# Turning SwiGLU's activation tiles with transposing transfers inside SBUF, with a reordered quad of weight sums and put-together steps set apart

## The chip, the cores and the metric

The kernel runs on one core of a Trainium2 chip. The metric is device time in microseconds of one execution, from launch to the last output. A core has five engines with a queue of instructions each, which run in order and wait for each other by semaphores: TensorE (PE; its weight loads are shown apart as PEld), VectorE (DVE), ScalarE (ACT), GpSimd (POOL) and SyncE (SP). Sixteen DMA engines move data between HBM and the on-chip memory SBUF, or inside SBUF; transfers are issued from the queues of SP, POOL and, rarely, ACT. TensorE writes its results to PSUM, eight banks of 128 x 512 float32.

## The reference

One layer of a decoder for 256 tokens of width 2048, all in float32. What surrounds the change is the SwiGLU feed-forward part (`D_FF` = 5632):

```python
h = rms_norm(x, g_ffn_pre[layer])
gate, up = jnp.split(h @ w_gate_up[layer], 2, axis=-1)
x = x + rms_norm((jax.nn.silu(gate) * up) @ w_down[layer], g_ffn_post[layer])
```

Before it stand a mixer (an input product `w_in` of sliding-window attention, a linear recurrence and two sigmoid gates, two branch products and `w_out`), after it a gated embedding (`w_ple_gate`). Every one of these is a product of 256 tokens with a weight matrix from HBM.

## The kernel before

The 256 tokens are two halves c = 0, 1 of 128. A product is made from blocks of 512 output columns, with the activation (turned, so that its 128-row groups k lie on the partitions) as the stationary operand and 128 x 512 pieces of the weights as the moving one. To get float32 accuracy, each operand is split into a rounded high part and a remainder, and `terms` (L473) makes three matmuls: high by high, low by high, high by low. So each weight piece that comes from HBM needs an ACT copy (`hi`, tile `wh`) and a DVE subtraction (`lo`, tile `wl`) before PE can use it.

The weights are loaded by SP in pairs (two row groups, 512 KB) in an order that `plan_of_weights` (L82) writes out. Two consecutive pairs, those of the same rows for two blocks of columns, form a quad. A quad is used in one of two ways. As usual it takes 2 x 2 x 2 products of three matmuls, 24 in all. A quad marked "seven" goes through seven products instead of eight (a Strassen-like scheme over the two row groups, the two token halves and the two blocks), 21 matmuls: `parts_of_quad` (L364) makes four sums t1 to t4 of weights on DVE and seven hi/lo splits, `in_place_of_quad` (L594) the sums on the side of the activation, and `by_quads` (L520) runs the products in the order b11, b21, t1, t2, b22, t4, t3. Four of the seven go to accumulators of their own (`sums`), which `put_together` (L567) combines after the last such quad of a block into four tiles u (one ACT copy `p1`, four DVE sums); `total` (L585) then adds each accumulator of the block to its u and frees the bank. During such a block all eight PSUM banks are in use: four accumulators and four sums.

In the gate/up stage, `swiglu(j)` (L1621) runs over eleven blocks j of 512 columns of gate and 512 of up. Block 0 is done in the plain way; j = 1 to 10 by quads, with four "seven" quads in blocks 2, 4, 6, 8, three in blocks 3, 5, 7, 9 and two in blocks 1 and 10 (`quads_of_block`, L61). At a block's end, for each half c, the gate's total goes through Silu on ACT, the up's total is multiplied by it on DVE, and `gated` (L1609) turns the resulting tile of 128 tokens x 512 columns, which must become four 128 x 128 groups with columns on the partitions: `transpose4` (L656) asks `misc` (L270) for a bank, which waits until at least three of the eight are free, and runs four PE transposes into it; ACT copies the bank to `actT`, and SP stores it to HBM (`actd`). During the `w_down` stage, `act_parts` (L1671) loads these tiles again through POOL's queue and splits them. `by_quads` and `put_together` are also used for two thirds of the gate columns of `w_in` (`gate_pair`, L1380), for half of `w_out`, and for `w_down`.

The order of the instructions on every queue is made by a small planner while the program is written. A clock advances with each matmul (0.227 us for one of 512 columns, 0.11 for a small one); `InOrder` (L154) estimates when DVE and ACT would be done with what they have been given (`until`). Work around the matmuls is written as generators: `yield T`, `yield A`, `yield V` ask to go on after that engine's planned end, `yield 0.5` after so much planned time, and `pump` (L219) resumes those that are due after each matmul group. `hurry` (L223) resumes them ahead of time when a bank or a tile is needed at once. `prefetch_quads` (L434) keeps at least two split weight items ready, or DVE planned 1.5 us ahead, as long as ten of the 61 SBUF slots (128 x 512 float32 each) are free. The planner's estimates only fix the order; on the chip the engines wait by semaphores.

Of the kernel before, what the change touches and what calls it, by code (L numbers as in the profile page):

```python
# [13 lines left out]
F32 = mybir.dt.float32  # L14
F32R = mybir.dt.float32r
I32 = mybir.dt.int32
AF = mybir.ActivationFunctionType
ALU = mybir.AluOpType
AX = mybir.AxisListType

P = 128
D = 2048
NB = 512
# [6 lines left out]

TABLES = (AF.Sigmoid, AF.Silu, AF.Exp, AF.Ln, AF.Sin)
TABLE_LOAD = 1.3
# [96 lines left out]
def block_kernel(ctx: ExitStack, tc: tile.TileContext, I, out: bass.AP):  # L129
# [24 lines left out]
    class InOrder:  # L154
# [20 lines left out]
        def __getattr__(self, name):  # L175
            f = getattr(self.engine, name)

            def call(o, *a, **kw):
                if name != "dma_start":
                    self.estimate(name, o, a, kw)  # L180
                return tc.keep_in_program_order(f(o, *a, **kw))  # L181

            return call

    V = InOrder(nc.vector, 0.07, 0.00105)
    A = InOrder(nc.scalar, 0.16, 0.0008)
    G, T, S = InOrder(nc.gpsimd, 0.9, 0.002), InOrder(nc.tensor, 0.0, 0.0), InOrder(nc.sync, 0.0, 0.0)
# [9 lines left out]
    def transpose(o, i, idn):  # L197
        clock[0] += SMALL
        T.transpose(o, i, idn)
# [29 lines left out]
    def nm(s):  # L229
        count[0] += 1  # L230
        return f"{s}_{count[0]}"
# [4 lines left out]
    def slot(s, shape=(P, NB), dt=F32):  # L236
        i = free_slots.popleft()
        t = slots.tile(list(shape), dt, tag=f"s{i}", name=nm(s))
        owner[id(t)] = i, t
        return t  # L240

    def free(*tiles):
        for t in tiles:
            free_slots.append(owner.pop(id(t))[0])

    def room(n):

        while len(free_slots) < n:
            yield 0.3
# [13 lines left out]
    def drop(ps):  # L263
        banks.append(bank_of.pop(id(ps))[0])
# [5 lines left out]
    def misc():  # L270
        while len(banks) < 3:
            yield 0.3
        return bank("misc")

    def act(o, i, f, **kw):
        return A.activation(o, i, f, **kw)

    def tt(o, a, b, op):
        return V.tensor_tensor(o, a, b, op)
# [12 lines left out]
    def cols(h, d=P):  # L292
        return slice(h * d, (h + 1) * d)
# [21 lines left out]
    def split_pair():  # L315
# [3 lines left out]
        if isinstance(raw, list):  # L319
            parts = [(slot("wh", dt=F32R), slot("wl", dt=F32R)) for j in range(2)]  # L320
            for (hi, lo), r in zip(parts, raw):
                act(hi, r, AF.Copy)
                tt(lo, r, hi.bitcast(F32), ALU.subtract)
            done = partial(free, *parts[0], *parts[1])
            free(*raw)
        elif len(in_pool) < SPLIT + 1:
            hi = wsplit.tile([P, 2, NB], F32R, tag="wh", name=nm("wh"))
            lo = wsplit.tile([P, 2, NB], F32R, tag="wl", name=nm("wl"))
            act(hi, raw, AF.Copy)
            tt(lo, raw, hi.bitcast(F32), ALU.subtract)  # L330
            parts, done = [(hi[:, j, :], lo[:, j, :]) for j in range(2)], in_pool.popleft
            in_pool.append(k)
        else:
            parts = [(slot("wh", dt=F32R), slot("wl", dt=F32R)) for j in range(2)]
            for j in range(2):
                act(parts[j][0], raw[:, j, :], AF.Copy)
            for j in range(2):
# [4 lines left out]
    def parts_of_pair():  # L342

        w, k, col, raw, _ = loaded.popleft()
        if len(in_pool) <= SPLIT:
            hi = wsplit.tile([P, 2, NB], F32R, tag="wh", name=nm("wh"))
            lo = wsplit.tile([P, 2, NB], F32R, tag="wl", name=nm("wl"))
            in_pool.append(k)
            act(hi, raw, AF.Copy)
            yield  # L350
            tt(lo, raw, hi.bitcast(F32), ALU.subtract)
            parts, done = [(hi[:, j, :], lo[:, j, :]) for j in range(2)], in_pool.popleft
        else:
            parts = [(slot("wh", dt=F32R), slot("wl", dt=F32R)) for j in range(2)]
            for j in range(2):
                act(parts[j][0], raw[:, j, :], AF.Copy)
            yield
# [6 lines left out]
    def parts_of_quad():  # L364

        w, k, col, raw, _ = loaded.popleft()
        other = loaded.popleft()[3]
        b11, b21, b12, b22 = raw[:, 0, :], raw[:, 1, :], other[:, 0, :], other[:, 1, :]
        parts = {}

        def hi(name, src):
            parts[name] = slot("wh", dt=F32R)
            act(parts[name], src, AF.Copy)

        def total(a, b, op):
            t = slot("t")
            tt(t, a, b, op)
            return t

        def lo(name, src):  # L380
            h, t = parts[name], slot("wl", dt=F32R)
            tt(t, src, h.bitcast(F32), ALU.subtract)
            parts[name] = h, t

        hi("b11", b11)
        hi("b21", b21)
        yield
        t1 = total(b11, b12, ALU.subtract)
        hi("t1", t1)
        lo("b11", b11)  # L390
        yield
        t2 = total(b22, t1, ALU.add)
        hi("t2", t2)
        t4 = total(b21, t2, ALU.subtract)
        hi("t4", t4)
        yield
        lo("b21", b21)
        load_more()
        t3 = total(b22, b12, ALU.subtract)
        hi("b22", b22)  # L400
        yield
        hi("t3", t3)
        lo("t1", t1)
        lo("b22", b22)
        load_more()
        free(t1)
        yield
        lo("t2", t2)
        lo("t4", t4)
        free(t2, t4)  # L410
        yield
        lo("t3", t3)
        free(t3)
        ready.append(((w, k, col), parts, None))

    def load_more():
        if plan:
            load_pair()
# [3 lines left out]
    def begin():  # L422

        if not loaded or len(making) > 1:
            return
        if loaded[0][4]:
            if len(loaded) > 1 and len(free_slots) >= STEP + SPARE:
                making.append(parts_of_quad())
                next(making[-1])
        elif len(in_pool) <= SPLIT or len(free_slots) >= ROOMY:  # L430
            making.append(parts_of_pair())
            next(making[-1])
# [87 lines left out]
    def by_quads(w, n, order, lhs, sides, cs, sums, us, start=True, stop=True, evac=None):  # L520
# [4 lines left out]
        for i, (q, seven) in enumerate(order):  # L525
# [38 lines left out]
            if last:  # L564
                chain(put_together(sums, us))

    def put_together(sums, us):  # L567

        yield T
        yield from room(4)  # L570
        p1, u2, u3, u4 = (slot("u") for _ in range(4))
        act(p1, sums["b11"], AF.Copy)
        drop(sums["b11"])
        yield A
        tt(u2, sums["t2"], p1, ALU.add)
        drop(sums["t2"])
        tt(u4, sums["t1"], u2, ALU.add)
        yield V
        tt(u3, sums["t3"], u2, ALU.add)
        drop(sums["t3"])  # L580
        tt(u2, sums["t1"], u3, ALU.add)
        drop(sums["t1"])
        us.extend([[p1, u3], [u4, u2]])

    def total(us, n, c, ps):  # L585
# [43 lines left out]
    def lookup(groups):  # L629
        def there(g):  # L630
            return g in groups if isinstance(groups, dict) else len(groups) > g and groups[g] is not None

        def f(k):
            hurry(lambda: there(k // 4))
            hi, lo = groups[k // 4]
            return hi[:, k % 4, :], lo[:, k % 4, :]
        f.groups = groups
        return f
# [17 lines left out]
    def transpose4(src):  # L656
        ps = yield from misc()
        for i in range(4):
            transpose(ps[:, cols(i)], src[:, cols(i)], ident)
        return ps  # L660
# [146 lines left out]
    sinks = amask[:, 256:272]  # L807
    posi = cst.tile([P, 2], I32, name="posi")

# [223 lines left out]
    def hgrn_core(c, g):  # L1033
# [55 lines left out]
        def scores(lev):  # L1089
# [22 lines left out]
            if lev < 5:  # L1112
                V.copy_predicated(
                    right(sc),
                    cmask[:, cols(lev, 64)].rearrange("p (n w) -> p n w", w=w).unsqueeze(1)
                    .broadcast_to([P, 4, nb, w]).bitcast(I32),
                    pv.rearrange("p h (n w) -> p h n w", w=w))
# [488 lines left out]
    stored, parts, sides, down_sides = [set(), set()], [], {}, {}  # L1606
    h2T = [lookup(n.groups) for n in norm2]

    def gated(c, j, t):  # L1609

        pa = yield from transpose4(t)
        free(t)
        yield T
        at = slot("actT")
        act(at, pa, AF.Copy)
        drop(pa)
        S.dma_start(actd[c][j], at)
        free(at)
        stored[c].add(j)

    def swiglu(j):  # L1621
# [16 lines left out]
        def ev_u(c, ps):  # L1638
            def f():
                if j in BY_QUADS and SEVEN:  # L1640
                    t = yield from total(us, 1, c, ps)
                    while sg[c] is None:
                        yield 0.3
                    yield sg[c]
                    stt(t, t, norm2[c].r, sg[c], ALU.mult, ALU.mult)
                    free(sg[c])
                else:
                    while sg[c] is None:
                        yield 0.3
                    t = sg[c]  # L1650
                    stt(t, ps, norm2[c].r, t, ALU.mult, ALU.mult)
                    drop(ps)
                yield V
                yield from gated(c, j, t)
            chain(f())
# [57 lines left out]
    for at, (pair, gi) in enumerate(DOWN):  # L1713
        if at % 5 == 0:
            ps, us = [[acc(), acc()] for n in range(2)], []
            sums = {"left": len(SEVEN_DOWN[pair])}
# [138 lines left out]
```

## Time and profile before

| | |
|---|---|
| three runs | 1487.32, 1487.96, 1491.14 us; median 1487.96 |
| the profiled execution | 1489.56 us, its span 1487.5 us |
| granted TensorE clock | 0.997 of full speed |
| busy: PE, DVE, ACT, POOL | 99%, 83%, 60%, 4% of the span |
| weights and other HBM reads | 298.08 MB, 211 GB/s over the span with the writes |
| the 22 tiles `actT` | first copied at 731.5 us, last at 1160.9 us |

The span counts from the first to the last recorded instruction; the execution's own time is about 2 us longer. The mean duration of one instruction is its time from start to end; since engines begin the next instruction before the last one has left the pipeline, the busy time of a group of back-to-back instructions is less than count times mean. In a group's row, "idle before" is the time that the engine stood still just ahead of these instructions, with what released it. All helpers record their instructions under one line, L181, so groups are told apart by engine and tile: `acc` are accumulators, `misc` banks for transposes and small products, `raw` weights as loaded, `wh` and `wl` their parts, `shi` and `slo` the parts of sums of activations, `t` sums of weights, `u` what put-together makes.

### The profile page before, as it was taken

What the parts mean: (1) busy time and instruction counts of PE and PEld (TensorE: products, weight loads), DVE (VectorE), ACT (ScalarE), POOL (GpSimd) and SP (SyncE); (2) the same over time, 40 slices, a digit from 0 to 9 for tenths busy, and PEclk for the clock granted to TensorE, in tenths of its full rate; (3) what the DMA queues carried; (4) which work ended last, traced back from release to release, by engine and by line L of the source; (5) the groups of instructions that cost most, each with busy time, mean ns of one, the idle gap of its engine ahead of it and who ended that gap; (6) DMA issues with size and microseconds to landing.
All of it is one profiled execution on the core that took longest, in us unless ns stands there. A gap on an engine that the chain in (4) does not pass through costs nothing.

```text
span 1487.5 us, 19958 instructions
## 1 busy us (share of the span) xinstructions
PE 1469.5 (99%) x6838; PEld 1216.3 (82%) x6838; DVE 1239.9 (83%) x2043; ACT 888.9 (60%) x1417; POOL 62.9 (4%) x107
## 2 busy tenths in 40 slices
PE   9999999999999999999999999999999999999997
PEld 6888888888887888888888888888888887888885
DVE  6878958755999867977899999999988899997773
ACT  7755655566666645665655666565655666575661
POOL 2100000000000100000000000000000000010000
PEclk9999999999999999999999999999999999999998
DMA  9754544345576856866756676576677678797551
GB/s 342 257 188 155 171 141 128 114 128 170 184 240 227 309 185 201 272 227 199 252 182 219 205 238 213 174 230 206 215 239 268 214 252 270 214 336 260 192 188 56
DMA packets 159557, 314.59 MB, mean 211 GB/s; under 512 B 11072, under 2 KB 11520, under 8 KB 159456
## 3 DMA queue, kind: packets, MB, share of 16 engines
q1 hardware_dynamic: 153024, 293.38, 61.0%
q0 software_dynamic: 6256, 19.88, 3.7%
q8 instruction: 53, 0.87, 0.2%
q14 instruction: 48, 0.39, 0.1%
q10 hardware_dynamic: 176, 0.07, 0.0%
HBM read 298.08 MB, written 15.21 MB: 211 GB/s over the span
## 4 chain that ended last, share of the span: by engine, by line
PE 64%; DVE 4%; issue 2%; DMA 1%; ACT 1%; DVEq 0%; POOLq 0%; POOL 0%; ACTq 0%
PE acc L181 63%; DVE wl L181 2%; PE misc L181 1%; DVE u L181 1%; ACT wh L181 1%; DVE t L181 1%; DMA raw<-in_w_in 1%; DMA raw<-in_w_down 0%; DMA raw<-in_w_gate_up 0%; DVE eg L181 0%; DVE slo L181 0%; DVE lo L181 0%; ACT hi L181 0%; DVE sides L181 0%; DVE s L181 0%
## 5 line engine op out<-in xcount | busy, mean ns | idle before, releaser
L181 PE MATMUL acc<-wh,hi 128*128 128x512 f32 x1769 | 700.2, 396 | 3.6 <-DVE u L181 2.4
L181 DVE TENSOR_TENSOR wl<-raw,wh 128x1024 fp32r<-128x1024 f32 (+1 forms) x606 | 595.7, 1007 | 115.4 <-ACT wh L181 113.8
L181 PE MATMUL acc<-wl,hi 128*128 128x512 f32 x1769 | 690.0, 390 | 0.0
L181 PE MATMUL acc<-wh,lo 128*128 128x512 f32 x1769 | 688.9, 389 | 0.0
L181 ACT ACTIVATE wh<-raw 128x1024 fp32r<-128x1024 f32 (+1 forms) x606 | 514.3, 883 | 239.8 <-PE acc L181 101.6
L181 PEld LDWEIGHTS acc<-wl,hi 128*128 128x128 f32 x1769 | 332.0, 188 | 71.2 <-DVE wl L181 1.1
L181 PEld LDWEIGHTS acc<-wh,hi 128*128 128x128 f32 x1769 | 332.3, 188 | 70.6 <-DVE u L181 3.2
L181 PEld LDWEIGHTS acc<-wh,lo 128*128 128x128 f32 x1769 | 332.5, 188 | 66.6 <-issue 0.2
L181 ACT ACTIVATE wh<-t 128x512 fp32r<-128x512 f32 x236 | 145.6, 628 | 106.6 <-DVE t L181 85.9
L181 DVE TENSOR_TENSOR wl<-t,wh 128x512 fp32r<-128x512 f32 x236 | 152.2, 683 | 0.5 <-PE acc L181 0.5
L181 DVE TENSOR_TENSOR u<-acc,u 128x512 f32<-128x512 f32 x132 | 86.3, 684 | 18.8 <-PE acc L181 17.6
L181 PE MATMUL acc<-wh,shi 128*128 128x512 f32 x236 | 91.9, 390 | 1.2 <-ACT shi L181 1.2
L181 PE MATMUL acc<-wh,slo 128*128 128x512 f32 x236 | 91.9, 390 | 0.2 <-DVE slo L181 0.2
L181 PE MATMUL acc<-wl,shi 128*128 128x512 f32 x236 | 91.8, 389 | 0.0
L181 DVE TENSOR_TENSOR t<-raw,t 128x512 f32<-128x512 f32 x118 | 81.1, 687 | 3.7
L181 PEld LDWEIGHTS acc<-wh,shi 128*128 128x128 f32 x236 | 44.3, 188 | 10.8 <-ACT shi L181 1.6
L181 PEld LDWEIGHTS acc<-wh,slo 128*128 128x128 f32 x236 | 44.3, 188 | 9.7 <-DVE slo L181 0.5
L181 PEld LDWEIGHTS acc<-wl,shi 128*128 128x128 f32 x236 | 44.3, 188 | 9.2
L181 POOL DMA_DIRECT2D act<-actd x40 | 21.4, 538 | 601.9 <-DVE wl L181 402.4
L181 DVE TENSOR_TENSOR t<-raw,raw 128x512 f32<-128x512 f32 x59 | 40.3, 684 | 3.9 <-DMA raw<-in_w_gate_up 1.9
L181 DVE TENSOR_TENSOR t<-raw 128x512 f32<-128x512 f32 x59 | 40.3, 684 | 0.0
L181 DVE TENSOR_TENSOR lo<-act,hi 128x512 fp32r<-128x512 f32 x40 | 27.2, 684 | 8.1 <-ACT hi L181 8.0
(214 smaller groups left out, 852.1 us busy)
## 6 DMA issues: line engine op xcount, KB each, us to landing
raw<-in_w_gate_up SPq DMA_DIRECT2D x176, 512.0 KB, 4.6
raw<-in_w_in SPq DMA_DIRECT2D x152, 512.0 KB, 4.3
raw<-in_w_down SPq DMA_DIRECT2D x88, 512.0 KB, 5.5
raw<-in_w_out SPq DMA_DIRECT2D x32, 512.0 KB, 5.5
raw<-in_w_ple_gate SPq DMA_DIRECT2D x32, 512.0 KB, 5.1
act<-actd POOLq DMA_DIRECT2D x40, 256.0 KB, 5.6
raw<-in_w_attn_branch SPq DMA_DIRECT2D x16, 512.0 KB, 5.2
raw<-in_w_hgrn_branch SPq DMA_DIRECT2D x16, 512.0 KB, 5.1
```

Source lines behind the costliest of these rows:

```text
L181: return tc.keep_in_program_order(f(o, *a, **kw))
```

## The change

It has three parts.

1. `gated` no longer uses PE and PSUM. ACT copies the tile, read as 16-bit halves, into a tile `apart` with all low halves first and all high halves after them (1024 two-byte elements per partition). ACT's queue issues one transposing transfer from SBUF to SBUF, which turns the eight 128 x 128 squares of halves into `turned`. After 7.0 us of planned time ACT copies the halves back together into `actT`; SP's store is now issued after ACT's planned end instead of at once. The input tile is freed as soon as `apart` has been written, without waiting for banks. The planner leaves transfers of either kind out of its estimates.
2. In `parts_of_quad`, the low part of b21 is made ahead of the sum t4 and its high part, instead of behind them and behind a pause.
3. In `put_together`, the four DVE sums are set apart by two planned pauses of 0.5 us where one pause lasted until DVE's planned end; the last u is t3 + u4 in place of t1 + u3, which is the same sum, so the bank of t1 is freed after the second sum and that of t3 after the fourth.

```diff
@@ class InOrder, call
-                if name != "dma_start":
+                if not name.startswith("dma_start"):
                     self.estimate(name, o, a, kw)
@@ parts_of_quad
         t2 = total(b22, t1, ALU.add)
         hi("t2", t2)
+        lo("b21", b21)
+        yield
         t4 = total(b21, t2, ALU.subtract)
         hi("t4", t4)
-        yield
-        lo("b21", b21)
         load_more()
@@ put_together
         tt(u2, sums["t2"], p1, ALU.add)
         drop(sums["t2"])
+        yield 0.5
         tt(u4, sums["t1"], u2, ALU.add)
-        yield V
+        drop(sums["t1"])
         tt(u3, sums["t3"], u2, ALU.add)
+        yield 0.5
+        tt(u2, sums["t3"], u4, ALU.add)
         drop(sums["t3"])
-        tt(u2, sums["t1"], u3, ALU.add)
-        drop(sums["t1"])
         us.extend([[p1, u3], [u4, u2]])
@@ gated
+    def halves(t):
+
+        return t.bitcast(U16).rearrange("p (n two) -> p two n", two=2)
+
     def gated(c, j, t):
 
-        pa = yield from transpose4(t)
+        apart = slot("apart", (P, 2 * NB), U16)
+        act(apart.rearrange("p (two n) -> p two n", two=2), halves(t), AF.Copy)
         free(t)
-        yield T
+        turned = slot("turned", (P, 8, P), U16)
+        A.dma_start_transpose(turned, apart)
+        free(apart)
+        yield 7.0
         at = slot("actT")
-        act(at, pa, AF.Copy)
-        drop(pa)
+        act(halves(at), turned.rearrange("p (two c) t -> p two (c t)", two=2), AF.Copy)
+        free(turned)
+        yield A
         S.dma_start(actd[c][j], at)
```

More of the change, by code (lines that the diff above doesn't have):

```diff
@@ L16 @@
 I32 = mybir.dt.int32
+U16 = mybir.dt.uint16
 AF = mybir.ActivationFunctionType
```

## The prediction

> **What bounds the kernel now.** I read the page's busy times first, then the groups of instructions for what TensorE waits on, then the chain, then the windows of the gate/up stage.
>
> ```profile
> span 1487.5 us, 19958 instructions
> PE 1469.5 (99%) x6838; PEld 1216.3 (82%) x6838; DVE 1239.9 (83%) x2043; ACT 888.9 (60%) x1417; POOL 62.9 (4%) x107
> L181 PE MATMUL acc<-wh,hi 128*128 128x512 f32 x1769 | 700.2, 396 | 3.6 <-DVE u L181 2.4
> ```
>
> TensorE (PE) is busy for 1469.5 of 1487.5 us; of the 18.0 us that are left, its largest matmul group waited only 3.6 us, 2.4 of them for VectorE (DVE) sums named u. So what leaves PE's stream leaves the time, as long as the engines that feed it keep up. Do they? Four blocks of the gate/up stage (those with four reordered quads, j = 2, 4, 6, 8), and the sum of ten windows of about a block each:
>
> ```profile
> 771.00:814.00 43.00, 43.00 (x191) 35.63 (x190) 41.19 (x59) 25.39 (x37) 0.00 (x0) 1.00 0.63 196
> 856.00:899.00 43.00, 43.00 (x195) 35.49 (x193) 41.17 (x60) 26.87 (x40) 0.00 (x0) 1.00 0.74 232
> 940.00:984.00 44.00, 44.00 (x199) 36.20 (x197) 42.58 (x62) 26.88 (x40) 0.00 (x0) 1.00 0.71 227
> 1025.00:1068.00 43.00, 43.00 (x196) 35.65 (x195) 41.73 (x60) 26.87 (x40) 0.00 (x0) 1.00 0.72 232
> sum 430.00, PE 429.54 PEld 355.09 DVE 401.77 ACT 258.35 POOL 5.38; mean PE 42.95 PEld 35.51 DVE 40.18 ACT 25.84 POOL 0.54
> ```
>
> Columns: window, length, busy time of PE, weight loads, DVE, ACT, POOL, then granted clock, share of the DMA engines, GB/s. PE is idle for 0.46 us in 430. DVE has 401.77 (93%), and in the blocks of four quads 41.2 of 43 to 42.6 of 44: no more than about 2 us behind PE. ACT has 60%, the DMA engines 63 to 74% in these blocks. PE bounds, DVE is close.
>
> **Term 1: the transposes leave PE.** Each of 22 activation tiles (11 blocks, 2 token halves) was turned by four PE transposes, 88 in all. A tile waits for three free banks, and a block holds all eight, so both halves' eight run together at a block's end. On the timeline and on the chain:
>
> ```profile
> 724.73 0.39 PE L181 MATMUL acc<-wh,hi 128*128 128x512 f32 x1
> ...
> 727.45 0.39 PE L181 MATMUL acc<-wh,hi 128*128 128x512 f32 x1
> ...
> 729.26 0.39 PE L181 MATMUL acc<-wl,hi 128*128 128x512 f32 x1
> 729.49 1.03 PE L181 MATMUL misc<-ident,sg 128*128 128x128 f32 x8
> 730.28 0.48 PE L181 MATMUL acc<-wh,hi 128*128 128x512 f32 x1
> 730.60 0.40 PE L181 MATMUL acc<-wh,lo 128*128 128x512 f32 x1
> ```
> ```profile
> 729.65 0.87 PE misc L181 x8
> ...
> 814.90 0.97 PE misc L181 x8
> ...
> 899.55 1.25 PE misc L181 x8
> ...
> 984.07 1.26 PE misc L181 x8
> ...
> 1068.57 1.11 PE misc L181 x8
> ...
> 1157.93 0.87 PE misc L181 x8
> ```
>
> A matmul starts every (727.45 - 724.73) / 12 = 0.227 us. Eight transposes take 730.28 - 729.49 = 0.79 us, and the first matmul after them is followed 0.32 us later instead of 0.227, so a group moves PE's stream by about 0.89 us. On the chain the eleven groups (shown are the first, the last and the four longest; the rest are 0.87 or 0.88) are 0.87 to 1.26 us each and sum to 10.7; the long ones hold a wait on a bank. Eleven times 0.89 is 9.8; counting the overlap with the next matmul, the groups' busy times sum to 12.1:
>
> ```profile
> L181 PE MATMUL misc<-ident,u 128*128 128x128 f32 x80 | 11.1, 277 | 0.5 <-DVE u L181 0.4
> L181 PE MATMUL misc<-ident,sg 128*128 128x128 f32 x8 | 1.0, 272 | 0.0
> L181 ACT ACTIVATE actT<-misc 128x512 f32<-128x512 f32 x22 | 12.5, 595 | 34.9 <-PE misc L181 34.9
> ```
>
> Bounds 9.8 and 12.1; I take the chain's 10.7, since the waits on a bank go with the transposes.
>
> **Term 2: ScalarE (ACT) gets more.** Out go 22 copies of 595 ns from PSUM, and 34.9 us in which ACT stood waiting for the transposes. In come, for each tile, a copy of 1024 two-byte elements that sets the halves apart, a DMA issue, and a copy of 1024 back. The nearest rows are the 1024-wide weight copy and the issues of plain transfers:
>
> ```profile
> L181 ACT ACTIVATE wh<-raw 128x1024 fp32r<-128x1024 f32 x367 | 380.2, 1055 | 218.1 <-PE acc L181 101.1 <-DMA raw<-in_w_down 37.2 <-DMA raw<-in_w_gate_up 36.3
> L181 ACTq DMA_DIRECT2D grow<-in_g_mix_pre x1: 494/494/494, 1.2 to 1.2; - x1
> ```
>
> 22 x (2 x 1.055 - 0.595) = 33.3 us, and 22 x 0.494 = 10.9 us of issuing. No row shows a transposing issue; 0.494 is the lower end, and twice to three times that the upper. ACT goes from 258 to about 302 us in a stage of 420: 72%, with 118 us idle, 5.4 per tile. Hidden behind PE, but not for free: behind each new copy in ACT's queue stand the weights' hi copies, on which DVE's lo parts and then PE depend. PE is covered by two ready pairs, 2 x 12 x 0.227 = 5.4 us, of which a pair's own hi and lo steps take 1.05 + 1.22 = 2.3 (the 1024-wide copy above, the row below), so a hold of ACT up to some 3.2 us costs nothing. I charge 0.5 us in all (0 to 5).
>
> ```profile
> L181 DVE TENSOR_TENSOR wl<-raw,wh 128x1024 fp32r<-128x1024 f32 x367 | 436.5, 1218 | 107.1 <-ACT wh L181 105.7 <-PE acc L181 1.1
> ```
>
> **Term 3: the new wait.** ACT's second copy waits for the transposing transfer; the code puts 7.0 us of planned time between issue and copy. How long 256 KB take here:
>
> ```profile
> act<-actd POOLq DMA_DIRECT2D x40, 256.0 KB, 5.6
> actd<-actT SPq DMA_DIRECT2D x22, 256.0 KB, 2.4
> x<-in_x SPq DMA_DIRECT2D x16, 256.0 KB, 7.4
> ```
>
> From 2.4 to 7.4 us; I take 5.6, the transfer issued in the midst of weight loads. That is under 7.0: no wait, and at 7.4 one of 0.4, inside the 3.2 us of cover. As load on the DMA engines, 22 x 2.4 = 53 us more in 430 raise a share of some 0.70 (the mean of the four rows of blocks above) to 0.82. Cost taken: 0. The other end is a rival below.
>
> The Trainium skill speaks against the change here: "VectorE: DVE Perf Modes", section "The three transpose paths", has 390 ns for a 128x128 square on TensorE and 1309 ns through the DMA crossbar, and its rules prefer TensorE where PSUM will do. "Advanced Engine Details and Errata", section "X-Bar Transpose (TRN2)", says that such transfers go as fast as regular ones, 350 to 400 GB/s. By the first, eight squares in sequence would be an estimated 10.5 us a tile, and 3.3 beyond the cover just worked out over eleven blocks, and terms 1 to 3 would sum to about -7; by the second 0.7 us, and term 3 stays 0. The trace shows neither, only that here a square costs PE 0.11 us.
>
> **Term 4: DVE in the blocks of four.** DVE gains and loses no instruction. If the four blocks cannot go faster than DVE, their shares of the gain (0.97, 1.25, 1.26 and 1.11 us of the eleven pieces, 4.6 together) come back as waits. Against that, a tile's slot is now free soon after the multiply instead of a whole block later, so DVE can run further ahead. Between 0 and +4.6 I take +1.5: DVE's 1 to 2 us of idle per block is about what is removed.
>
> **Term 5: put-together steps and the reordered quad.** These touch the gate branch, w_out, gate/up and w_down alike. The put-together steps (16 of them, one PSUM copy and four DVE sums each) are made after fixed pauses of 0.5 us instead of behind DVE's planned end, so other lo steps may come between, but the totals behind them, which free banks, can be emitted earlier. What it can win is PE's wait for u, 2.4 us by the first group row. The count of steps and the price of a sum:
>
> ```profile
> L181 ACT ACTIVATE u<-acc 128x512 f32<-128x512 f32 x16 | 9.3, 578 | 0.0
> L181 DVE TENSOR_TENSOR u<-acc,u 128x512 f32<-128x512 f32 x132 | 86.3, 684 | 18.8 <-PE acc L181 17.6
> ```
>
> What it can lose is one lo step (86.3 / 132 = 0.65 us for a sum of the same size) at a few places where PE is close behind, say three, so -2.4 to about +2; I take -1.0. In the quad, lo of b21 moves ahead of t4: t4's hi comes one DVE step later, but PE uses t4 sixth, behind five products of 3 x 0.227 = 0.68 us, 3.4 us of cover, while b21 is used second. Taken: 0; without that cover 0.65 us per quad. The store of the turned tile is now issued once ACT is due to have finished. SyncE held it, and the weight loads behind it, for this long:
>
> ```profile
> SPq L181 <- ACT actT L181: 77.7, 16, 10.5
> ```
>
> Loads may start earlier, but PE in this stage is not waiting for loads: 0.
>
> **Sum.** -10.7 + 0.5 + 0 + 1.5 - 1.0 = -9.7 us. The profiled execution took 1489.56 us (span 1487.5, 2.1 around it), so 1479.9 for that one; the median of the three runs is 1487.96, 1.6 lower, which gives 1478.3 us. A difference under 0.3% (4.5 us) counts as no change, that being what a measurement of this kernel can tell.
>
> **Rival A, slower: the transposing transfer is late and ACT stands.** It decides when a transfer takes longer than 7.0 + 3.2 = 10.2 us from issue to landing: from there on PE waits, once per block, since the two halves' transfers overlap. The gain is used up at 10.2 + 9.7 / 11 = 11.1 us. Taking two of the longest 256 KB landings one after the other, 14.8 us, it costs 11 x 4.6 = 51: 1529 us; at 12 us, 11 x 1.8 = 20: 1498. For it: no such transfer in this trace, and the DMA engines are already two thirds busy. Against it: the longest plain landing of this size is 7.4. The 1309 ns of the VectorE page (10.5 us a tile, an estimate) would come just short of deciding. Chance 0.13.
>
> **Rival B, no change: DVE becomes the bound.** The four blocks give back 4.6, and in the others ACT's 44 us more delay hi copies, so that DVE's idle of 1 to 2 us per block is not usable; another 3 us come back. -10.7 + 4.6 + 3 is -3: 1485 us. For it: DVE at 93% in the stage, 96 to 97% in blocks of four, and the long chain pieces sit at the ends of just those. Against it: DVE was kept from its work partly by waits on PE. Chance 0.19.
>
> **Rival C, more:** all bank waits vanish too, -12.1 - 2.4: 1473.5 us. For it: the waits at block ends are on banks that the transposes also took. Chance 0.05, within "faster".
>
> **Numbers.** Forecast 0.63 (1475 to 1483). Faster 0.68, same 0.19, slower 0.13. From 1474 to 1490 lies about 8 in 10: it takes in the forecast and Rival B, and leaves out most of A and of C.
>
> **What would show it.** Right: no PE rows on misc in 728 to 1158 us, PE busy lower by 10 to 12 us with its idle under 20, ACT up by about 45 us, the wait of ACT's second copy for its transfer below 1 us in the mean. Wrong: a PE wait for ACT or DVE at block starts of about 1 us each (B), a landing above 10 us and ACT idle on it, DMA share near 0.9 in the stage (A), or new waits on u in the gate branch (term 5).

## The result and the profile after

| | before | after |
|---|---|---|
| median, us | 1488.01 | 1494.47 |
| runs, us | 1487.32 to 1491.14 (8) | 1490.99 to 1496.56 (8) |
| profiled execution, its span, us | 1489.56, 1487.5 | 1490.99, 1489.2 |
| granted TensorE clock in it | 0.997 | 0.996 |

The ratio after to before is 1.0037, with a 95% interval of 1.0025 to 1.0048: slower by a little more than the 0.3% that the prediction called no change, and outside its range of 1474 to 1490 us. The profiled execution of after is the fastest of its eight, so its rows show rather too little of the loss.

The page of after, the lines that answer to those of before (in a group's row: busy us, mean ns | idle us before, what released it):

```profile
span 1489.2 us, 19825 instructions
...
PE 1464.4 (98%) x6750; PEld 1209.2 (81%) x6750; DVE 1239.0 (83%) x2044; ACT 918.1 (62%) x1440; POOL 62.9 (4%) x107
...
L182 PE MATMUL acc<-wh,hi 128*128 128x512 f32 x1769 | 701.9, 397 | 9.9 <-DVE u L182 9.4
```

The 88 transposes are gone (6838 to 6750 matmuls), yet PE is busy only 5.1 us less, and it is idle for 24.8 us (1489.2 - 1464.4) instead of 18.0. Nearly all of that new idle time is in one group: 9.9 us instead of 3.6, and 9.4 of it until a DVE sum u is done. Where? The same four blocks as in the prediction (PE, weight loads, DVE, ACT, POOL busy; clock, DMA share, GB/s):

```profile
771.00:814.00 43.00, 42.25 (x186) 34.35 (x185) 40.71 (x58) 29.13 (x41) 0.00 (x0) 1.00 0.73 222
856.00:899.00 43.00, 41.06 (x180) 33.39 (x179) 40.90 (x60) 29.97 (x43) 0.00 (x0) 1.00 0.71 223
940.00:984.00 44.00, 42.04 (x185) 34.13 (x184) 41.87 (x61) 29.97 (x43) 0.00 (x0) 1.00 0.70 219
1025.00:1068.00 43.00, 41.34 (x180) 33.55 (x180) 40.50 (x59) 29.65 (x43) 0.00 (x0) 1.00 0.72 224
```

PE was busy without a break in them before; now it loses 0.75, 1.94, 1.96 and 1.66 us. But DVE does less than before as well (163.98 us over the four, 166.67 before), so DVE is not the bound: it waits too. The waits of the stage (window 728 to 1110 us; in total, times, longest), first before, then after:

```profile
DVE wl L181 <- ACT wh L181: 1.7, 3, 0.7
```
```profile
DVE wl L182 <- ACT wh L182: 17.3, 20, 1.6
...
PE acc L182 <- DVE u L182: 8.6, 10, 2.1
```

DVE's lo steps stand 17.3 us for ACT's hi copies instead of 1.7. DVE has 4 to 7% of spare time here, so a block's last lo steps and the sums behind them come late, and PE stands for u at the block's end. A block's end in after, on DVE's timeline (first line) and on the chain that ended last (start, length, what):

```profile
1064.41 0.69 DVE L182 TENSOR_TENSOR wl<-raw,wh 128x512 fp32r<-128x512 f32 x1 [0.84 <-ACT wh L182]
...
1065.02 3.02 DVE wl L182 x4
1068.04 0.61 DVE u L182
1068.65 0.04 issue
1068.69 3.50 PE acc L182 x10
```

From 1029 us on DVE had waited for hi three times, 2.1 us in all, the wait of 0.84 us last; then come four lo steps and the sum u, and PE, which stood for 2.09 us, starts 0.04 us behind u. ACT's timeline at another block's end in after (start, length, engine):

```profile
774.67 1.04 ACT L182 ACTIVATE apart<-u 128x1024 uint16<-128x1024 uint16 x1
775.74 1.25 ACTq L182 DMA_TRANSPOSE turned<-apart  x1
777.10 1.06 ACT L182 ACTIVATE wh<-raw 128x1024 fp32r<-128x1024 f32 x1 [1.38 <-PE acc L182]
778.06 1.04 ACT L182 ACTIVATE apart<-u 128x1024 uint16<-128x1024 uint16 x1
779.13 1.26 ACTq L182 DMA_TRANSPOSE turned<-apart  x1
```

From 774.67 to 780.39 us (779.13 + 1.26) ACT makes one hi copy; the rest is two copies that set halves apart and two issues. The releaser "PE acc" in the third row had long been done: the gap of 1.38 us is the issue. And the transfer itself, by the view of the tile `turned`:

```profile
L182 ACTq DMA_TRANSPOSE turned<-apart x22: 1247/1249/1332, 730.7 to 1163.8; - x22
L182 ACT ACTIVATE actT<-turned x22: 1337/1362/1377, 735.6 to 1173.4; 128x1024 uint16<-128x1024 uint16 x22
its engine sat idle before it (us, times) until:
  DMA turned<-apart: 0.3, 1
...
DMA to landing us min/median/max: 2.7/4.4/9.6
```

An issue takes 1.25 us, the copy back 1.36; the transfer lands after 4.4 us in the median, and this copy waited for it 0.3 us in all. Nor is ACT held up more by weight loads: from 728 to 1160 us its hi copies wait 35.7 us for them in after and 53.8 in before.

The longest stall costs more than its length. PE's timeline and two windows behind it, after:

```profile
1068.69 0.50 PE L182 MATMUL acc<-wh,hi 128*128 128x512 f32 x1 [2.09 <-DVE u L182]
...
1070.28 0.63 PE L182 MATMUL acc<-wh,hi 128*128 128x512 f32 x1
1070.71 0.63 PE L182 MATMUL acc<-wh,lo 128*128 128x512 f32 x1
```
```profile
1070.00:1072.00 2.00, 2.00 (x7) 1.51 (x6) 1.90 (x3) 0.00 (x0) 0.00 (x0) 0.53 0.59 219
1072.00:1074.00 2.00, 2.00 (x7) 1.63 (x6) 2.00 (x4) 0.00 (x0) 0.00 (x0) 0.62 0.00 0
```

After 2.09 us of idle time the granted clock falls to a mean of 0.53 and 0.62 in these windows of 2 us, and matmuls start 0.43 us apart instead of 0.227: some eight of them, 8 x 0.2 = 1.6 us more. The same happens once behind a wait of 1.89 us at 1219 us, in the `w_down` stage.

### The profile page after: what moved, and what is told of

It is laid out like the page before. It is cut to its first block, busy times and chain, and to the rows that moved or that the text cites. A ratio compares the mean times of both kernels' runs of the same rounds, so it can differ in the third digit from the quotient of the medians.

```text
span 1489.2 us, 19825 instructions
## 1 busy us (share of the span) xinstructions
PE 1464.4 (98%) x6750; PEld 1209.2 (81%) x6750; DVE 1239.0 (83%) x2044; ACT 918.1 (62%) x1440; POOL 62.9 (4%) x107
## 4 chain that ended last, share of the span: by engine, by line
PE 84%; DVE 8%; issue 3%; ACT 2%; DMA 2%; ACTq 0%; SPq 0%; DVEq 0%; POOLq 0%; POOL 0%
PE acc L182 79%; PE misc L182 5%; DVE wl L182 4%; ACT wh L182 2%; DVE u L182 2%; DVE t L182 1%; DMA raw<-in_w_gate_up 1%; DMA raw<-in_w_ple_proj 1%; DMA raw<-in_w_in 0%; ACTq L182 0%; ACT apart L182 0%; DVE eg L182 0%; DVE lo L182 0%; SPq L182 0%; ACT actT L182 0%
## 5 line engine op out<-in xcount | busy, mean ns | idle before, releaser
L182 DVE TENSOR_TENSOR wl<-t,wh 128x512 fp32r<-128x512 f32 x236 | 152.9, 685 | 10.8 <-ACT wh L182 7.0
```

## The experiments

Three groups: what each part does alone, what in the turning costs, and which of ACT's holds it is. All kernels were timed in five rounds beside the kernel before, whose median was between 1487.73 and 1488.63 us. "DVE for hi" and "PE idle" are from the window 728 to 1110 us of each kernel's profiled execution (the wait of wl for wh; 382 less PE's busy time), which is one execution only: the slowest of its kernel in e5, e9, e18 and e20, the fastest in after, e1, e8, e11, e13 and e19. "ACT at issues" is 22 times the mean time, on ACT's timeline, from the end of the instruction ahead of a transfer's issue to the start of the next one. The kernels ran on several chips, each beside before, so that two of them are compared more fairly by the ratios than by the medians: the ratios put after 16.2 us above e5 (0.0109 x 1488), the medians 17.9.

| kernel | median us | ratio [95%] | ACT at issues | DVE for hi | PE idle |
|---|---|---|---|---|---|
| before | 1488.01 | 1 | none | 1.7 | 0.5 |
| after | 1494.47 | 1.0037 [1.0025, 1.0048] | 30 | 17.3 | 8.6 |
| e1 turning alone | 1492.36 | 1.0036 [1.0024, 1.0048] | 30 | 10.8 | 5.1 |
| e2 both sums edits alone | 1494.31 | 1.0047 [1.0034, 1.0060] | none | 18.0 | 6.3 |
| e16 put-together alone | 1493.77 | 1.0043 [1.0028, 1.0058] | none | 15.3 | 6.2 |
| e17 quad alone | 1490.96 | 1.0018 [1.0008, 1.0027] | none | 14.0 | 3.2 |
| e4 turning and put-together | 1495.70 | 1.0057 [1.0045, 1.0069] | 30 | 13.8 | 9.0 |
| e5 nothing turned | 1476.58 | 0.9928 [0.9916, 0.9940] | none | 1.8 | 0.0 |
| e7 copies, no transfer | 1478.76 | 0.9933 [0.9921, 0.9945] | none | 9.2 | 0.9 |
| e8 transfer, not read | 1478.83 | 0.9942 [0.9928, 0.9956] | 20 | 2.0 | 0.0 |
| e9 SP issues | 1480.33 | 0.9942 [0.9930, 0.9955] | none | 3.8 | 1.4 |
| e13 SP issues, old sums | 1479.60 | 0.9944 [0.9932, 0.9955] | none | 1.6 | 0.0 |
| e14 SP issues, b11 first | 1479.89 | 0.9945 [0.9933, 0.9957] | none | 5.8 | 3.1 |
| e10 copies on POOL | 1520.89 | 1.0218 [1.0205, 1.0231] | none | 0.7 | 25.3 |
| e11 pause, ACT issues | 1490.87 | 1.0015 [1.0006, 1.0024] | 5 | 6.9 | 5.8 |
| e12 halves 5 us apart | 1503.39 | 1.0101 [1.0087, 1.0115] | 31 | 18.0 | 12.8 |
| e15 SP issues, ACT held | 1484.22 | 0.9974 [0.9964, 0.9985] | none | 8.5 | 3.7 |
| e18 plain transfer | 1480.75 | 0.9954 [0.9940, 0.9968] | 13 | 10.3 | 2.6 |
| e19 e9, slot freed later | 1481.50 | 0.9957 [0.9943, 0.9972] | none | 8.5 | 2.5 |
| e20 e11, slot freed later | 1479.62 | 0.9938 [0.9925, 0.9951] | 7 | 10.5 | 5.2 |

### The parts alone

e1 keeps only part 1 of the diff, e2 only parts 2 and 3, e4 leaves out part 2 (their edits are the diff's own lines, undone). e5 is after without any turning:

```diff
@@ e5, gated
-        apart = slot("apart", (P, 2 * NB), U16)
-        act(apart.rearrange("p (two n) -> p two n", two=2), halves(t), AF.Copy)
+        at = slot("actT")
+        act(at, t, AF.Copy)
         free(t)
-        turned = slot("turned", (P, 8, P), U16)
...
-        free(turned)
         yield A
```

> Part 1 alone: the transposing transfers, with the quad and the put-together steps as before. Three theories of where the 10.7 us of PE transposes went. H: ACT is held 3.65 us per tile (two copies of 1.04 and 1.36 us and 1.25 us of issuing, against 0.60 before), hi copies come late, DVE and then PE wait; then this one is as slow as the changed kernel, 1492 to 1496 us. D: DVE is at its limit in the blocks of four quads, so PE only meets it sooner and waits for its sums u; then also about 1488 to 1495, with the waits for u at the starts of blocks. P: the pauses of 0.5 us put the four put-together sums and the four totals in one row on DVE at a block's end; then without them the forecast gain is there, 1478 to 1482.

> Parts 2 and 3 without part 1: the reordered quad and the spaced put-together steps, with PE transposes as before. P: slower than before by the loss and the wait on u, 1490 to 1496 us. H and D: within 2 us of before, 1486 to 1490.

> Parts 1 and 3, the quad as before. All three theories leave the quad out: 1492 to 1496 us, as the changed kernel. If it is under 1489, the low part of b21 ahead of t4 is what costs.

> The changed kernel without any turning (the tile is copied by one 512-wide ACT copy and stored unturned, so the output is not the reference's): PE is free of transposes, and ACT has 0.62 us per tile in place of 3.65. H: the whole gain shows, 1476 to 1481 us. D: PE still waits for u at block starts, 1485 to 1492. P: as D, since the put-together steps are the changed ones.

e5, by its page:

```profile
span 1477.8 us, 19745 instructions
...
PE 1461.2 (99%) x6750; PEld 1209.0 (82%) x6750; DVE 1237.6 (84%) x2045; ACT 883.9 (60%) x1419; POOL 62.9 (4%) x107
...
L182 PE MATMUL acc<-wh,hi 128*128 128x512 f32 x1769 | 699.7, 396 | 0.8 <-DVE u L182 0.4
```

With nothing in their place, the transposes are worth 11.2 us (1487.73, the median of before beside it, less 1476.58), or 0.72% by the ratio (0.60 to 0.84), with parts 2 and 3 still in the kernel. The wait for u shrinks to 0.4 us and PE is never idle in the stage: DVE keeps up with the shorter blocks. So what after loses against e5, 17.9 us of the medians, comes from the turning's own steps. In the profiled executions (1490.99 and 1479.58) the loss is 11.4: idle time 24.8 against 16.6, and busy time 1464.4 against 1461.2. About 1.7 of these last 3.2 us are a stretch of low clock, of which after has two and e5 one, behind a wait of 2.28 us at 1228 us; the rest is open.

Turning alone (e1) is as slow as the whole change. Parts 2 and 3 alone cost as much, 0.47%, but by another way, which e16 and e17 divide; and the costs don't add.

> The kernel before with the spaced put-together steps alone. Parts 2 and 3 together cost 6.6 us with PE transposes. If the put-together steps do it (four sums and four totals in one row, ahead of the lo parts of the next quad): 1492 to 1496. If the quad: 1486 to 1489.

> The kernel before with the reordered quad alone: the low part of b21 ahead of t4. If the put-together steps cost: 1486 to 1490. If the quad does: 1491 to 1496.

Both are before with one edit of the diff, part 3 in e16 and part 2 in e17. DVE stands for hi in either, 15.3 and 14.0 us. In e16 behind the end of block 4 (ACT's timeline, then DVE's):

```profile
911.38 1.08 ACT L181 ACTIVATE actT<-misc 128x512 f32<-128x512 f32 x2 [5.10 <-PE misc L181]
```
```profile
913.02 0.69 DVE L181 TENSOR_TENSOR wl<-t,wh 128x512 fp32r<-128x512 f32 x1 [3.33 <-ACT wh L181]
```

ACT's copies of turned tiles wait 5.10 us for PE's transposes, with hi copies behind them in the queue, and DVE runs dry for 3.33. The edits change the order that the planner writes, and in it such a copy stands ahead of hi copies that are needed sooner. One block's end shows this. In the whole stage, though, ACT waits for transposes about as long in before (27.5 us) as in e16 (31.6) and e17 (23.8), so what differs would be what stands behind these waits. That this is the whole cost, or that the pauses or the earlier drops as such bring it, is argued only.

### What in the turning costs

e7 makes both copies but no transfer (the copy back reads `apart`). e8 is e5 with a transposing transfer from ACT's queue that nobody reads. e9 issues the transfer on SP once ACT is due to have finished, and e13 is e9 with parts 2 and 3 undone. e14 is e9 with the four sums in the order b11, t1, t2, t3. e10 makes both copies on GpSimd.

```diff
@@ e7, gated
-        turned = slot("turned", (P, 8, P), U16)
-        A.dma_start_transpose(turned, apart)
-        free(apart)
         yield 7.0
         at = slot("actT")
-        act(halves(at), turned.rearrange("p (two c) t -> p two (c t)", two=2), AF.Copy)
-        free(turned)
+        act(halves(at), apart.rearrange("p (two n) -> p two n", two=2), AF.Copy)
+        free(apart)
@@ e8, gated
+        turned = slot("turned", (P, 8, P), U16)
+        A.dma_start_transpose(turned, t.bitcast(U16))
+        at = slot("actT")
+        act(at, t, AF.Copy)
         free(t)
+        yield 7.0
+        free(turned)
```
```diff
@@ e9, gated
         free(t)
+        yield A
         turned = slot("turned", (P, 8, P), U16)
-        A.dma_start_transpose(turned, apart)
+        S.dma_start_transpose(turned, apart)
```
```diff
@@ e14, by_quads, beside the lines of e9
-("t1", "t2", "t3", "b11")
+("b11", "t1", "t2", "t3")
@@ e10, gated, beside the lines of e9
-        act(apart.rearrange("p (two n) -> p two n", two=2), halves(t), AF.Copy)
+        G.tensor_copy(apart.rearrange("p (two n) -> p two n", two=2), halves(t))
```

> The changed kernel with both ACT copies of 16-bit halves but no transfer between them (the tile is stored unturned, so the output is not the reference's). Without any turning the kernel took 1476.6 us, with it 1494.5: 17.9 us to share out. H1, ACT's copies (1.04 + 1.36 us against 0.62 per tile): 1486 to 1494. H2, ACT's 1.25 us of issuing per tile: 1476 to 1480. H3, the transposing transfer's load on the DMA engines delays the weights: 1476 to 1480.

> The kernel without turning, and beside it one transposing transfer per tile, issued by ACT, whose result nobody reads (the tile is copied once, 512 wide, and stored unturned). H1: 1476 to 1480. H2 and H3: 1484 to 1494.

> The changed kernel with the transposing transfers issued by SyncE, after ACT's planned end, in place of ACT: 27.5 us less on ACT's queue, the same on SP's, ahead of weight loads. H2: 1477 to 1486. H1: 1488 to 1493. H3: 1492 to 1497, as the transfers stay.

> SP issues, and the quad and the put-together steps are as before (part 1 alone, with SP). Parts 2 and 3 cost 6.6 us with PE transposes and 1 to 3 with ACT issuing. If they cost by themselves: 1473 to 1478. If they only cost where DVE is late, and otherwise win the 1.6 to 2.4 us of waits in the gate branch: 1481 to 1484.

> SP issues, and of the four banks for a block's seven-products the first one freed goes to b11, which PE uses first, in place of the last one. If the waits for u at the blocks' starts that are left (about 1 us in the gate/up stage, 0.4 in the gate branch) are on the last total's bank: 1478 to 1480.5, a gain of up to 1.5. If PE waits elsewhere: 1480 to 1482.

> As with SyncE issuing, and both copies of halves on GpSimd in place of ACT, which then has nothing to do for the turning. H1 and H2: 1474 to 1482, unless GpSimd's copies slow DVE or come too late. H3: 1488 or more.

By the medians above e5, the copies cost 2.2 us (1478.76 - 1476.58), the transfer 2.2 (1478.83), and copies, transfer and the reading of its result together, with SP issuing, 3.7 (1480.33); by the ratios 0.7, 2.1 and 2.1. The intervals of all four kernels overlap, so none of these costs is clear of noise; all are small beside after's. e7 rules out the copies as the sole cause, and e8 the issue on ACT, or the transfer's load, as the sole cause: each was expected to bring most of the loss if it were. The transfers stay in e9, which speaks against their load once more. Some 14 us of after's 17.9 go when the issue leaves ACT's queue behind a pause; e11, below, has the pause without SP. The wait rows of e9, from 728 to 1110 us:

```profile
DVE wl L182 <- ACT wh L182: 3.8, 8, 0.9
...
PE acc L182 <- DVE u L182: 1.0, 1, 1.0
```

With the issue on SP, parts 2 and 3 do nothing that can be measured (e9 0.9942, e13 0.9944, between the two outcomes that were expected), nor does the order of the sums (e14). GpSimd is the wrong place for the copies: its copies are slow, and DVE's steps beside them too (`wl<-t,wh` takes 685 ns in the mean over the whole run of after, 747 here):

```profile
L182 POOL COPY apart<-u 128x1024 uint16<-128x1024 uint16 x20 | 70.7, 3556 | 292.0 <-DVE u L182 200.0 <-PE acc L182 92.0
L182 POOL COPY actT<-turned 128x1024 uint16<-128x1024 uint16 x22 | 40.8, 1884 | 54.9 <-DMA turned<-apart 48.9 <-PE acc L182 5.9
```

### Which hold of ACT it is

First attempts: e11 puts a pause between the first copy and the issue, so that the planner can set other work between them; e12 sets the second half's tile 5 us later, so that the two tiles' holds don't come back to back.

```diff
@@ e11, gated
         free(t)
+        yield A
         turned = slot("turned", (P, 8, P), U16)
@@ e12, gated
+        if c == 1:
+            yield 5.0
         apart = slot("apart", (P, 2 * NB), U16)
```

> The changed kernel, ACT issuing, with the one other thing that the kernel with SP issuing had: a pause until ACT's planned end between the first copy and the issue. If the engine that issues is what matters (H2): 1488 to 1496 us. If it was the order of the program that the pause changes: 1477 to 1484, as with SP.

> The changed kernel with the second token half's copy and issue 5.0 us of planned time later, so that ACT is held twice for 2.3 us instead of once for 4.6. Theory HOLD: a hold beyond the cover of some 3 us is what costs, which is why copies alone and transfers alone cost 2 us each and both together 18: 1478 to 1486. Theory SUM: ACT's time as such (67 us more in the stage) costs: 1491 to 1496.

e12 is a miss: 1503.39 us, the slowest order with these copies on ACT. Over its whole run ACT stood 12.9 us, in four waits, for transfers that landed 9.6 us after issue at most, and DVE 9.4 for slots that a transfer had still to read; from 728 to 1110 us DVE also stood 18.0 for hi. So the theory that the two tiles' holds cost because they come back to back isn't borne out: set apart, they brought other and longer waits. e11 gains 3.6 us on after, less than hoped, though the issue itself is nearly free in it. PE's, DVE's and ACT's instructions stand in the same order in e11 as in e9, so the 10.5 us between these two come with the queue that issues. ACT's timeline in e11:

```profile
772.87 1.04 ACT L182 ACTIVATE apart<-u 128x1024 uint16<-128x1024 uint16 x1
773.82 1.04 ACT L182 ACTIVATE wh<-raw 128x1024 fp32r<-128x1024 f32 x1
773.94 1.25 ACTq L182 DMA_TRANSPOSE turned<-apart  x1
775.29 1.06 ACT L182 ACTIVATE apart<-u 128x1024 uint16<-128x1024 uint16 x1 [0.43 <-PE acc L182]
```

The issue at 773.94 runs beside the copy of 773.82. In after the issue stands right behind the copy whose result it sends and can't begin before that copy ends, so ACT does nothing else meanwhile: 1.36 us each, 30 us in all; in e11 0.22 us each. What e11 has instead, by its waits over the whole run:

```profile
DVE wl L182 <- DMA turned<-apart: 6.9, 4, 3.5
DVE t L182 <- DMA turned<-apart: 5.9, 3, 2.5
```

DVE stands 12.8 us until a transfer has read its source. `free(apart)` is at the issue, so the planner hands the slot to the next weight tile, and its writer must wait for the transfer. Four more kernels tell these apart. e18 is after with a plain transfer in place of the transposing one; in the two traces PE's, DVE's and ACT's instructions stand in the same order. e15 is e9 with two copies of nothing on ACT (junk, 1.27 us together) behind each issue, which the planner doesn't count. e20 is e11, and e19 is e9, with the slot of `apart` freed after the pause of 7.0 us.

```diff
@@ e18, gated
-        A.dma_start_transpose(turned, apart)
+        A.dma_start(turned.rearrange("p a b -> p (a b)"), apart)
@@ e15, gated, beside the lines of e9
         S.dma_start_transpose(turned, apart)
+        for _ in range(2):
+            tc.keep_in_program_order(nc.scalar.activation(
+                junk.rearrange("p (a b) -> p a b", a=4), ident.unsqueeze(1).broadcast_to([P, 4, P]), AF.Copy))
@@ e19 and e20, gated
-        free(apart)
         yield 7.0
+        free(apart)
```

> The kernel with SP issuing (1480.3 us), and on ACT, where the issue stood, two ACT copies of nothing that is used (512 elements each, about 1.2 us together), which the planner does not see. If ACT's time as such is what the issue costs: 1486 to 1492, near the 1490.9 of the kernel with the same order and ACT issuing. If it is something else in issuing from ACT's queue (the transfer's place behind ACT's own copy, its queue): 1479 to 1483.

> The changed kernel with a plain transfer from SBUF to SBUF, issued by ACT, in place of the transposing one (the tile is stored unturned, so the output is not the reference's). If the 1.25 us of a transposing issue against about 0.4 to 0.5 of a plain one is what holds ACT: 1479 to 1486. If any transfer that ACT issues behind its own copy costs as much: 1491 to 1496.

> SP issues, and the slot of the halves set apart is given back only with ACT's second copy, 7.0 us of planned time later. With the slot given back at once, DVE waited 6.2 us for transfers, to write into that slot. If these waits reach PE: 1476 to 1479. If PE is covered against them: 1479 to 1482.

> The kernel with the pause and ACT issuing (1490.9 us, DVE waited 12.8 us for transfers), with the slot given back late in the same way. A dummy hold of ACT of the same length without a transfer gave 1484.2. If the slot's waits are the 6.7 us between: 1482 to 1486. If they are not: 1489 to 1492.

The view of `turned` in e18, and the place on ACT's timeline that was shown for after:

```profile
L182 ACTq DMA_DIRECT2D turned<-apart x22: 472/472/510, 732.3 to 1155.2; - x22
...
DMA to landing us min/median/max: 2.2/2.7/5.0
```
```profile
774.80 1.04 ACT L182 ACTIVATE apart<-u 128x1024 uint16<-128x1024 uint16 x1
775.87 0.47 ACTq L182 DMA_DIRECT2D turned<-apart  x1
776.44 1.06 ACT L182 ACTIVATE wh<-raw 128x1024 fp32r<-128x1024 f32 x1 [0.60 <-PE acc L182]
```

- e18 against after: the same order, an issue of 0.47 us in place of 1.25 and a landing of 2.7 in place of 4.4. Its median is 13.7 us lower (12.4 by the ratios). In after, ACT waited only 1.1 us for transfers (0.3 with the copy back, 0.8 with a hi copy) and DVE not at all, and ACT's waits for weight loads are much the same (35.7 us from 728 to 1160 us in after, 31.5 in e18). So it is the issue: ACT stands 13 us at the issues instead of 30.
- e20 against e11: the edit frees the slot later, and the planner's order changes with it. The 12.8 us of waits are gone and the median falls by 11.3 us, to 1479.62, below either of the expectations, with an issue on ACT still taking 1.25 us in the median. e19 has the very order of e20 with SP issuing, and its interval overlaps e20's. So an issue on ACT is not dear in itself; in after's order, right behind its own copy, it is. In e19 the later freeing takes away 6.2 us of such waits and gains nothing (1481.50 against 1480.33, intervals overlap), so it is not the waits in total that count but where they fall.
- e15: 27.4 us more on ACT, about what after spends at its issues, cost 3.9 us (4.8 by the ratios) and not 14, between the two outcomes that were expected. The same amount of ACT's time at other places of the order is worth a third of that or less.

e20, e13, e14 and e9, which leave nothing out, are 0.55 to 0.62% faster than before and 3 to 4 us above e5.

## Why the prediction was wrong

**Term 1 (-10.7) was right.** e5 measures 0.72%, 10.7 us of 1488 (8.9 to 12.5 by the interval, so that the agreement to a tenth is luck), and bears out the reading that what leaves PE's stream leaves the time.

**Term 2 is the step that failed:** "Hidden behind PE, but not for free ... I charge 0.5 us in all (0 to 5)". It came to about 14 to 16 us: the 16.2 (by the ratios) to 17.9 (by the medians) by which after lies above e5, less the 2 or so that e8 gives for the transfer. Of its prices, the first copy was right (1.04 us against 1.055), the copy back was 1.36, and the issue was near the upper end that the text had set, 1.25 against two to three times 0.494. What was wrong is the cover, "a hold of ACT up to some 3.2 us costs nothing". It was counted for one hold, met with two ready pairs, and for PE's wait on split weights. But PE stood on the sums u at the blocks' ends (8.6 us in ten waits), which DVE makes behind its late lo steps, and the cover says nothing of these. A tile's first copy and issue hold ACT for 2.43 us (774.67 to 777.10), below 3.2, and yet DVE waited 20 times, never longer than 1.6 us: many short waits where none was expected. So DVE had no two pairs of hi copies in hand at those places, and, 93% busy, it made up little afterwards of what it had stood. The price is steep: ACT's copies with a plain transfer cost some 4 us (e18 above e5), and the longer issue 12 to 14 more. Why the same time at other places costs a third or less (e15), and why setting the tiles 5 us apart costs more (e12), is not settled: e15 stands in e9's order and not in after's, and e12's edit also changes what the planner orders next. Shown is that the issue's length at its place in after's order makes most of the loss (e18), and that a kernel rearranged so that most issues run beside other copies, with the slot held until the copy back, does not have it (e20).

**Term 3 (0) was about right.** ACT waited 0.3 us; the landing was 4.4 us in the median where 5.6 was taken. The transfer with its issue cost about 2 (e8), not clear of noise, and the DMA share in the blocks was 0.70 to 0.73, not 0.82: the estimate took the whole time to landing as load on all engines. The Trainium skill's 1309 ns for a square through the crossbar ("VectorE: DVE Perf Modes", "The three transpose paths") had given an estimate of 10.5 us a tile; the trace doesn't agree, eight squares land in 4.4. Nor does "as fast as regular" ("Advanced Engine Details and Errata", "X-Bar Transpose (TRN2)") hold for this size: the plain transfer of the same tile lands in 2.7 us, and 0.8 of the difference is the longer issue.

**Term 4 (+1.5) and Rival B fall as to their cause.** DVE as the bound gives nothing back: with nothing turned, PE has no idle time in the stage. Rival B did name ACT's delay of hi copies, "another 3 us come back", and this is what happened, at some five times the size and without its other half.

**Term 5 (-1.0) was wrong in sign taken alone.** The wait of 1.59 us that PE had in the gate branch at 468 us is gone in after, as argued. But the two edits by themselves cost 0.47% (e2). At the block's end shown for e16 the way led through ACT's copies standing for PE's transposes, which the prediction did not look at: it priced no more than lo steps in DVE's queue. On top of the turning they add nothing (e1 and after, 1.0036 and 1.0037), so the sum did not fail by them.

**Rival A did not happen in after.** A weaker form did in e12: ACT stood 12.9 us for transfers, though none took more than 9.6 us where Rival A set 10.2, and the kernel was slower by 1.0%, with DVE's waits in it too. The forecast's side was wrong for a reason that none of the rivals priced.

Of the signs that were to show it right, no transposes and a wait for the transfer below 1 us came true, PE's busy time fell by 5.1 us instead of 10 to 12, and its idle time was not under 20. Of the signs that were to show it wrong, Rival B's came true: PE waits for DVE at block starts, 0.86 us each in the mean. ACT's busy time grew by 29 us, not 45, in part because issuing isn't counted as busy; the 30 us at the issues come on top, and that is the part that hurt.

## What to carry to other kernels

Cost a DMA issue as time of the engine that issues it, and look at what stands ahead of it: right behind the instruction whose result it sends it can't overlap (1.36 us lost each in after), while behind other copies already queued it can (0.2 to 0.3 us in e11 and e20). It does so only as long as these run: in e8, where the next copy follows at once, ACT still stood 0.9 us per issue. An engine with 40% idle time has little cover when its output feeds an engine that is 93% busy; ask what the fed engine has in hand at that place, not how much idle time there is in all. And try the bound first: a kernel that leaves the new work out (e5) shows what there is to gain and that the loss is in the new steps.

## What was not expected of the hardware

- **The clock gate can take less than expected.** In after, idle times of 2.09 and 1.89 us were followed, 1.3 to 1.6 us after PE's restart, by about 3.5 us at a granted clock of 0.53 to 0.62; idle times of 1.69 and 1.68 us were not. But the length alone does not decide: in e15 one of 1.63 us was followed by such a stretch, and in e20 ones of 2.13 and 2.61 us and in e12 one of 3.07 us were not. The Trainium skill ("TensorE: Matmul & The Clock Gate", "Part 1: The HAM clock gate") puts the fall after an idle window of about 3.4 us that runs freely; in these traces a wait of about half that can be followed by it.
- **A transposing issue holds its queue for 1.25 us** in the median, on ACT and on SP, where a plain one of the same 256 KB takes 0.47 us on ACT.
- **A copy of 1024 two-byte elements on ACT** takes 1.04 us when the read is strided and 1.36 us when the write is.
